# Transposed products with x: both parts of x in one instruction, the halves added by the taker

## The chip, the cores and the metric

The kernel runs as one program on one core of a Trainium2 chip. Its time is the device time of one execution, in microseconds (us). The time before is the median of three runs; the profile comes from one more execution. The engines are PE (TensorE: matrix products), DVE (VectorE), ACT (ScalarE), POOL (GpSimd) and SP (SyncE, which starts transfers).

## The reference

The kernel computes four layers over 256 tokens of width 1024, one batch, all in fp32. The first block has two layers alike, each of a SwiGLU, a mixer and a second SwiGLU, with a layer norm behind each part. The second block has a layer with an S5 mixer and pooling, and one with stick-breaking attention, each followed by a mixture of 16 experts. Cut to what matters here:

```python
def swiglu(x, w_in, w_out):
    h = x @ w_in
    gate, up = h[..., :D_FF], h[..., D_FF:]          # D_FF = 2816
    return (jax.nn.silu(gate) * up) @ w_out

def hybrid_mixer(x, ...):
    h = x @ w_in                                     # dq dk dv sq sk sv
    ...                                              # rope on q and k
    y_diff = diff_attention(dq, dk, dv, ...)         # softmax(..0) - lam * softmax(..1), times v
    y_swa = swa_sink_attention(sq, sk, sv, ...)      # softmax with a sink in a window of 128
    return concatenate([y_diff, y_swa], -1) @ w_out

def first_block(x, ...):
    for l in range(2):
        x = layer_norm(ALPHA * x + 0.5 * swiglu(x, ...), ...)
        x = layer_norm(ALPHA * x + hybrid_mixer(x, ...), ...)
        x = layer_norm(ALPHA * x + 0.5 * swiglu(x, ...), ...)
    return x
```

## The kernel before

**Products in parts.** Each fp32 operand is split into two parts of a shorter type (fp32r), a rounded one (hi) and the rest (lo), and a product a·b is the sum of hi·hi, hi·lo and lo·hi, added up in PSUM. A weight unit is 256 columns of a weight matrix by all 1024 rows: it is loaded by SP into a ring, ACT rounds it (L336) and DVE subtracts to get the rest (L337). The transposed x lies in two tiles, xh and xl (8 x 256 columns each for the eight slices k of 128 rows).

**S and T.** `S` (L386 to L388) computes 128 output columns by 256 tokens, transposed: for each k three matmuls of 256 columns, hi·xh, hi·xl and lo·xh, into one half of a PSUM bank. A unit has two such parts (m = 0, 1), which share one bank. `T` (L399 to L401) multiplies the FFN's inner tile with rows of the second weight: 12 matmuls of 512 columns a round, into four banks of their own (bank_acc). All other products take banks of one pool of four, bank_w, in turn; a bank is reused when its last reader is done.

**FFN.** There are 22 tiles of 128 inner columns. Rounds i = 2 to 20 go the same way in all four FFNs: S for the gate and the up half of tile i, silu on ACT (L574), multiply on DVE (L575), rounding on ACT (L516) and the rest on DVE (L517), and T for tile i-1 on PE. The rows of the second weight are split on ACT and DVE (L373, L378). PE's order is S(i), T(i-1), S(i+1). On DVE the subtractions for unit i+1 (L337) come ahead of the multiply of round i. FFN 4 (the second of layer 2, 860 to 1025 us) carries in its rounds also the preparation of the S5 layer, mostly small operations on DVE and, late, some products on PE. The tail of the FFN handles the last tile token by token (L543, L544, L549).

**Mixer.** Five units go through S (`proj`) and a copy from the bank into a tile qs on ACT (L795, `proj_out`); then rope: one matmul on PE (L803), multiplies on POOL and DVE (L807). Between the projections stand the softmax of the sliding window (scores L829, maximum L842, normalizing L851), the transposes of the probabilities (L817, `at_T`, evacuated on DVE by L114) and their products with v (L860). The order of the calls is written out by hand, and each engine works through its queue in that order.

**Stick-breaking layer.** Eight units go through S (`qk`) and one scaled copy on ACT (L2155).

The S5 layer's tile gyhl and the experts' tile ple lie in the buffers of xl, plain transposed x in that of xh.

Of the kernel before, what the change touches and what calls it, by code (L numbers as in the profile page):

```python
# [8 lines left out]
F32 = mybir.dt.float32  # L9
F32R = mybir.dt.float32r  # L10
BF16 = mybir.dt.bfloat16
I32 = mybir.dt.int32
AF = mybir.ActivationFunctionType
ALU = mybir.AluOpType
# [3 lines left out]
P = 128  # L18
D = 1024
# [63 lines left out]
class K:  # L83
# [117 lines left out]
                between = between()  # L201

    def new_plain_xT(self, xT=None):
        self.xT = xT or self.xp.tile([P, 8, 256], F32, tag="xh", name="xT")

    def new_xT(self):
        self.xh = self.xp.tile([P, 8, 256], F32R, tag="xh", name="xh")
        self.xl = self.xp.tile([P, 8, 256], F32R, tag="xl", name="xl")

    def load_ln(self, g, b):  # L210
        t = self.lp.tile([P, 2, D], F32, tag="lnrow", name="lnrow", bufs=1)
# [166 lines left out]
        (lo_eng or self.nc.vector).tensor_sub(lo, src, f(hi))  # L378
        return hi, lo

    def S(self, out, unit, m):

        hi, lo = unit
        for k in range(8):
            a, b = hi[:, m, k, :], lo[:, m, k, :]
            self.nc.tensor.matmul(out, a, self.xh[:, k, :], start=(k == 0), stop=False)  # L386
            self.nc.tensor.matmul(out, a, self.xl[:, k, :], start=False, stop=False)  # L387
            self.nc.tensor.matmul(out, b, self.xh[:, k, :], start=False, stop=(k == 7))  # L388

    def T(self, acc, st, unit, first, last, tts=(0, 1), hs=(0, 1)):  # L390

# [114 lines left out]
    def ffn(self, row, next_pre, hooks={}):  # L506
        nc = self.nc
        sp = self.sp
        acc = None
        rows = {}  # L510
        queue = []
        new_g = lambda: sp.tile([P, 2, 256], F32R, tag="rt", name="gg", bufs=3)
        new_s = lambda: sp.tile([P, 2, 256], F32, tag="qs", name="sg", bufs=3)

        def split_g(gg, cols, src):
            nc.scalar.copy(gg[:, 0, cols], src)  # L516
            nc.vector.tensor_sub(gg[:, 1, cols], src, f(gg[:, 0, cols]))  # L517

        def down(last=False):
            nonlocal acc  # L520
            i, gg = queue.pop(0)
            if acc is None:
                acc = self.new_acc()
            self.T(acc, (gg[:, 0], gg[:, 1]), rows.pop(i), i == 0, last)
            if i + 2 < NF:
                rows[i + 2] = self.ffn_rows(i + 2)


        u = list(self.pre)
        g2 = [new_g() for _ in range(2)]  # L530
        tok = {}

        def proj(j, tt):
            b = self.bank()[:, :256]
            self.proj_T(b, u[j], tt)
            return b

        def head(j, tt, b=None):
            if b is None:
                b = proj(j, tt)  # L540
            sg = new_s()
            s, g = sg[:, 0, :P], sg[:, 1, :P]
            nc.scalar.activation(s, b[:, 0:P], AF.Silu)  # L543
            nc.vector.tensor_mul(g, s, b[:, P:256])  # L544
            tok[j, tt] = g

        def head_tr(j, tt):
            b = self.bank()[:, :P]
            nc.tensor.transpose(b, tok.pop((j, tt)), self.ident)  # L549
            split_g(g2[j], slice(tt * P, tt * P + P), b)  # L550

        head(0, 0, self.hb[0])
        b01 = proj(0, 1)
        head(1, 0, self.hb[1])
        rows[0] = self.ffn_rows(0)
        head_tr(0, 0)
        head(0, 1, b01)
        head_tr(1, 0)
        nxt = self.ffn_cols(2)
        head(1, 1)  # L560
        rows[1] = self.ffn_rows(1)
        head_tr(0, 1)
        queue += [(0, g2[0]), (1, g2[1])]
        for i in range(2, NF - 1):
            unit = nxt
            nxt = self.ffn_cols(i + 1)
            pg = self.bank()
            for m in range(2):
                self.S(pg[:, m * 256:m * 256 + 256], unit, m)
            if i == 2:  # L570
                head_tr(1, 1)
            sg = new_s()
            s, g = sg[:, 0], sg[:, 1]
            nc.scalar.activation(s, pg[:, 0:256], AF.Silu)  # L574
            nc.vector.tensor_mul(g, s, pg[:, 256:512])  # L575
            gg = new_g()
            split_g(gg, slice(0, 256), g)
            queue.append((i, gg))
            while len(queue) > (2 if i == 2 else 1):
                down()  # L580
            if i in hooks:
                hooks[i]()

        u[0] = nxt
        g2[0] = new_g()
        _, gg = queue.pop()
        before, last = rows.pop(NF - 2), rows.pop(NF - 1)
        units = []

        def part(g, r, tt, h, end):  # L590
            self.T(acc, (g[:, 0], g[:, 1]), r, False, end, (tt,), (h,))

        def over0():
            units.append(self.in_steps(next_pre[0]))
            units[0]("copy", 0.75)
            units[0]("sub", 0.5, nc.gpsimd)

        def over1():
            units[0]("copy")
            units[0]("sub", 1, nc.gpsimd)  # L600
            units[0]("free")
            head(0, 1)
            part(gg, before, 1, 0, False)

        def over2():
            units.append(self.in_steps(next_pre[1]))
            head_tr(0, 1)
            units[1]("copy", 0.25)
            part(gg, before, 1, 1, False)

        def over3():
            units[1]("sub", 0.25, nc.vector)

        def over4():
            part(g2[0], last, 1, 0, True)
            return over4_2

        def over4_2():
            units[1]("copy")
            units[1]("sub", 0.25, nc.gpsimd)  # L620
            part(g2[0], last, 1, 1, True)

        def over5():
            units[1]("sub", 0.25, nc.gpsimd)
            units[1]("sub", 1, nc.vector)
            units[1]("free")

        head(0, 0)
        part(gg, before, 0, 0, False)
        head_tr(0, 0)  # L630
        part(gg, before, 0, 1, False)
        for h in range(2):
            part(g2[0], last, 0, h, True)
        self.layer_norm(acc, True, row() if callable(row) else row, done=self.head,
                        over=(over0, over1, over2, over3, over4, over5))
# [149 lines left out]
        yield u  # L785

    def proj(self, unit):
        b = self.bank()
        for m in range(2):
            self.S(b[:, m * 256:m * 256 + 256], unit, m)  # L790
        return b

    def proj_out(self, b):
        qs = self.sp.tile([P, 2, 256], F32, tag="qs", name="qs", bufs=3)
        self.nc.scalar.copy(qs.rearrange("p m t -> p (m t)"), b)  # L795
        return qs

    def rope(self, qs, dst, cos, sin):
# [561 lines left out]
    def s5_layer(self, wk, sc, projected, row, head, scanned):  # L1360

        nc = self.nc
        V, G = nc.vector, nc.gpsimd
        mm = nc.tensor.matmul
# [7 lines left out]
        S = [sc.tile([P, 2, 4, 65], F32, name=f"S{i}") for i in range(4)]  # L1372
# [173 lines left out]
        vproj(1, 1)  # L1546
        projected()
        scan(3)
        yhl = self.xp.tile([P, 2, 4, 256], F32R, tag="xl", name="gyhl")
        yh, yl = yhl[:, 0], yhl[:, 1]  # L1550
        for g in range(4):
            pooled(g)
        for g in range(4):
# [29 lines left out]
        g = self.rows_units()  # L1583
# [3 lines left out]
        for mp in range(2):  # L1587
            b = self.bank()
            for m in range(2):
                o = b[:, m * 256:m * 256 + 256]  # L1590
                for k in range(4):
# [8 lines left out]
                                   op0=ALU.add, op1=ALU.mult)  # L1600
# [94 lines left out]
    def moe_head(self, l):  # L1695


        nc = self.nc
        mm = nc.tensor.matmul

        class H:
# [15 lines left out]
            def proj(h, tt, halves=(0, 1)):  # L1717

                if tt == 0 and 0 in halves:
                    self.ple = self.xp.tile([P, 2, D], F32, tag="xl", name="ple")  # L1720
                    h.ip, W = self.ring.take()
                    h.pw = W[:, :2 * D].rearrange("p (k c) -> p k c", k=2)
                out = []
                for i in halves:
                    c, op = slice(512 * i, 512 * i + 512), self.bank()
                    out.append((c, op))
                    for k in range(2):
                        mm(op, h.pT[:, k, tt * P:tt * P + P], h.pw[:, k, c], start=(k == 0), stop=(k == 1))
                if tt == 1 and 1 in halves:
                    self.ring.free(h.ip)  # L1730

                def rest():
                    for c, op in out:
                        nc.scalar.activation(self.ple[:, tt, c], op, AF.Copy, scale=0.5)
                return rest
# [388 lines left out]
    def sb_layer(self, wk, sc, projected, row, head, scored):  # L2124

        nc = self.nc
        V, G = nc.vector, nc.gpsimd
        mm = nc.tensor.matmul
        v = sc.tile([P, 2, D], F32, name="sbv")
        yh = wk.tile([P, 8, 256], F32R, name="sbyh")  # L2130
# [17 lines left out]
        vproj(3, 1)  # L2148

        def qk(unit, scale):  # L2150
            b = self.bank()
            for m in range(2):
                self.S(b[:, m * 256:m * 256 + 256], unit, m)
            t = sc.tile([P, 2, 256], F32, tag="qk", name="qk", bufs=6)
            nc.scalar.activation(t.rearrange("p m t -> p (m t)"), b, AF.Copy, scale=scale)  # L2155
            return t

        def scores(q, k, m):
# [322 lines left out]
```

## Time and profile before

| what | us |
|---|---|
| three runs | 1792.59, 1797.18, 1796.63 |
| median | 1796.63 |
| the profiled execution | 1793.23 |
| its span | 1791.5 |
| busy in the span: PE, DVE, ACT, POOL | 1704.7, 929.0, 712.7, 348.2 |
| S: 4512 matmuls of 256 columns | 1270.6 |

The profiled execution is 1.7 us longer than its span, which runs from the first to the last recorded instruction. Busy time is the sum of an engine's records, of which those of PE overlap one another: a matmul's record reaches past the start of the next. So the distance between starts tells how long a stream of matmuls takes, and the mean of a record does not. A share of busy time is a mean over stages of different kinds; the windows and timelines below look at single stages. The mean clock granted to PE in the profiled execution was 0.989 of full speed.

### The profile page before, as it was taken

Reading aid. Unit: us, or ns where it says so; the run is one execution under the profiler, and the core shown is the slowest. Engines: PE = TensorE matmul, PEld = TensorE weight load, DVE = VectorE, ACT = ScalarE, POOL = GpSimd, SP = SyncE. Lnnn points to the kernel's source line nnn. Section 1 sums busy time; section 2 is a strip of 40 time slices with the busy share of each in tenths; the row PEclk is TensorE's granted clock in tenths of the full one; section 3 lists DMA queues with packets and bytes.
Section 4 is the critical chain, followed back from the end, with each engine's and each line's share of the span. In section 5 each row is a group of like instructions: output and inputs, shape, how many; then the busy total and the mean of one; then the engine's idle time right before and its main releaser. Section 6 shows DMA issues by size and latency. Waiting matters only on the chain. (4 is left out here: it accounts for less than half of the span.)

```text
span 1791.5 us, 27789 instructions
## 1 busy us (share of the span) xinstructions
PE 1704.7 (95%) x11407; PEld 1328.9 (74%) x11407; DVE 929.0 (52%) x1523; ACT 712.7 (40%) x1256; POOL 348.2 (19%) x403
## 2 busy tenths in 40 slices
PE   9999998999999999998999988899998999899997
PEld 7999886899989998867999887445453987445443
DVE  5654677655475546677677776432222534422223
ACT  5444456444454444465444435312111465212111
POOL 1000464200020002637061064200000213100001
PEclk9999999999999999999999999999999999999999
DMA  8755442565646555525454556699998737599994
GB/s 286 226 186 195 148 135 87 172 210 167 211 150 209 177 194 165 150 87 153 154 200 152 194 198 257 235 414 414 410 420 322 244 133 289 222 414 414 411 419 184
DMA packets 189483, 421.45 MB, mean 235 GB/s; under 512 B 7264, under 2 KB 142736, under 8 KB 165280
## 3 DMA queue, kind: packets, MB, share of 16 engines
q1 hardware_dynamic: 184848, 405.82, 62.4%
q0 software_dynamic: 3920, 12.95, 2.5%
q8 instruction: 94, 1.54, 0.4%
q10 hardware_dynamic: 576, 0.77, 0.1%
q14 instruction: 45, 0.37, 0.1%
HBM read 418.47 MB, written 1.05 MB: 234 GB/s over the span
## 5 line engine op out<-in xcount | busy, mean ns | idle before, releaser
L386 PE MATMUL bank_w<-xh,unit 128*128 128x256 f32 x1504 | 425.8, 283 | 0.5 <-DVE sg L575 0.5
L388 PE MATMUL bank_w<-xh,unit 128*128 128x256 f32 x1504 | 422.6, 281 | 0.1
L387 PE MATMUL bank_w<-xl,unit 128*128 128x256 f32 x1504 | 422.2, 281 | 0.0
L337 DVE TENSOR_TENSOR unit<-ring,unit 128x1024 fp32r<-128x1024 f32 (+2 forms) x220 | 270.4, 1266 | 51.4 <-ACT unit L336 47.3
L386 PEld LDWEIGHTS bank_w<-xh,unit 128*128 128x128 f32 x1504 | 283.2, 188 | 4.5 <-issue 1.0
L387 PEld LDWEIGHTS bank_w<-xl,unit 128*128 128x128 f32 x1504 | 283.4, 188 | 3.1 <-issue 0.5
L388 PEld LDWEIGHTS bank_w<-xh,unit 128*128 128x128 f32 x1504 | 283.3, 188 | 0.3 <-DVE unit L337 0.3
L336 ACT CAST unit<-ring 128x1024 fp32r<-128x1024 f32 (+2 forms) x297 | 248.5, 891 | 11.1 <-DMA ring<-in_ffn_w_in_dram 10.9
L337 POOL TENSOR_TENSOR unit<-ring,unit 128x512 fp32r<-128x512 f32 (+1 forms) x77 | 113.3, 1488 | 628.9 <-ACT unit L336 628.9
L1902 PE MATMUL bank_w<-ring,xg 128*64 128x512 f32 x1024 | 223.2, 593 | 0.0
L378 DVE TENSOR_TENSOR rl<-ring,rh 128x1024 fp32r<-128x1024 f32 x104 | 129.8, 1249 | 167.3 <-ACT rh L373 167.0
L1902 PEld LDWEIGHTS bank_w<-ring,xg 128*64 128x64 f32 x1024 | 74.2, 137 | 139.8 <-issue 139.0
L373 ACT CAST rh<-ring 128x1024 fp32r<-128x1024 f32 x108 | 113.1, 1049 | 110.2 <-PE bank_acc L401 110.2
L399 PE MATMUL bank_acc<-rh,gg 128*128 128x512 f32 x352 | 139.3, 396 | 0.0
L401 PE MATMUL bank_acc<-rh,gg 128*128 128x512 f32 x352 | 138.5, 394 | 0.0
L400 PE MATMUL bank_acc<-rl,gg 128*128 128x512 f32 x352 | 138.4, 393 | 0.0
L1952 PE MATMUL bank_w<-ring,hT 128*64 128x512 f32 x512 | 113.4, 595 | 2.1 <-issue 2.1
L1916 DVE CAST ohT<-bank_w 128x256 fp32r<-128x256 f32 x16 | 6.8, 425 | 191.9 <-PE bank_w L1912 191.9
L259 POOL TENSOR_SCALAR s_ld<-s_m,s_mu 128x1 f32<-128x1 f32 x20 | 16.6, 832 | 434.0 <-DVE s_mu L250 433.9
L574 ACT ACTIVATE sg<-bank_w 128x256 f32<-128x256 f32 x76 | 29.2, 384 | 172.5 <-PE bank_w L388 172.5
L1952 PEld LDWEIGHTS bank_w<-ring,hT 128*64 128x64 f32 x512 | 38.0, 137 | 68.3 <-issue 66.7
L1960 ACT CAST yhl<-bank_w 128x512 fp32r<-128x512 f32 x32 | 18.7, 586 | 147.3 <-PE bank_w L1952 147.3
(502 smaller groups left out, 2592.2 us busy)
## 6 DMA issues: line engine op xcount, KB each, us to landing
ring<-in_moe_w_dram SPq DMA_DIRECT2D x188, 1024.0 KB, 13.8
ring<-in_ffn_w_in_dram SPq DMA_DIRECT2D x86, 1024.0 KB, 6.6
ring<-in_ffn_w_out_dram SPq DMA_DIRECT2D x44, 1024.0 KB, 5.1
ring<-in_w_in_dram SPq DMA_DIRECT2D x18, 1024.0 KB, 5.8
ring<-in_sb_w_qkv_dram SPq DMA_DIRECT2D x12, 1024.0 KB, 11.3
ring<-in_ple_w_gate_dram SPq DMA_DIRECT2D x8, 1024.0 KB, 18.1
ring<-in_w_out_dram SPq DMA_DIRECT2D x8, 512.0 KB, 6.1
ring<-in_w_out_dram SPq DMA_DIRECT2D x4, 1024.0 KB, 5.2
```

The costliest lines, as they stand in the source:

```text
L336: copy = lambda sel=sel, src=src: self.nc.scalar.copy(sel(hi), src)
L337: sub = lambda eng=eng, sel=sel, src=src: eng.tensor_sub(sel(lo), src, f(sel(hi)))
L373: (copy or self.nc.scalar.copy)(hi, src)
L378: (lo_eng or self.nc.vector).tensor_sub(lo, src, f(hi))
L386: self.nc.tensor.matmul(out, a, self.xh[:, k, :], start=(k == 0), stop=False)
L387: self.nc.tensor.matmul(out, a, self.xl[:, k, :], start=False, stop=False)
L388: self.nc.tensor.matmul(out, b, self.xh[:, k, :], start=False, stop=(k == 7))
L399: mm(acc[tt][h], a, hi[:, cols], start=first, stop=False)
L400: mm(acc[tt][h], a, lo[:, cols], start=False, stop=False)
L401: mm(acc[tt][h], b, hi[:, cols], start=False, stop=last)
L1902: nc.tensor.matmul(b[64 * e:64 * e + 64], xg[:, 4 * kh + k, c0 + 64 * e:c0 + 64 * e + 64], ws[e][0][:, 512 * k:512 * k + 512], start=(kh = ...
L1952: nc.tensor.matmul(yb[h][64 * e:64 * e + 64], hT[:, jj, 64 * e:64 * e + 64], w, start=(jj == 0), stop=(jj == 3))
```

## The change

`S` takes a whole bank per part m. Per k it issues one matmul of 512 columns, hi times both parts of x side by side, and one of 256 columns, lo·xh, added into the bank's first half. The bank then holds two halves, whose sum is the result. Who takes the result adds them: `halves` copies the second half on ACT and adds the first on DVE. FFN: two such pairs per round ahead of silu and multiply, which now read SBUF; mixer: two pairs in place of one copy; stick-breaking: two scaled copies on ACT and two multiply-adds on DVE in place of one scaled copy. The tiles xh and xl become one tile xx, so that one instruction can read both, and the tiles that shared their buffers move into it. 94 units (76 in the FFNs, 10 in the mixers, 8 in the stick-breaking layer) go through S, each with 2 parts of 8 k.

```diff
@@ -201,11 +201,16 @@
                 between = between()
 
     def new_plain_xT(self, xT=None):
-        self.xT = xT or self.xp.tile([P, 8, 256], F32, tag="xh", name="xT")
+        if xT is None:
+
+            t = self.xp.tile([P, 2, 2048], F32, tag="xx", name="xTs")
+            self.sums = t[:, 1].rearrange("p (t c) -> p t c", t=2)
+            xT = t[:, 0].rearrange("p (k t) -> p k t", k=8)
+        self.xT = xT
 
     def new_xT(self):
-        self.xh = self.xp.tile([P, 8, 256], F32R, tag="xh", name="xh")
-        self.xl = self.xp.tile([P, 8, 256], F32R, tag="xl", name="xl")
+        self.xx = self.xp.tile([P, 2, 8, 256], F32R, tag="xx", name="xx")
+        self.xh, self.xl = self.xx[:, 0], self.xx[:, 1]
 
     def load_ln(self, g, b):
         t = self.lp.tile([P, 2, D], F32, tag="lnrow", name="lnrow", bufs=1)
@@ -378,14 +383,21 @@
         (lo_eng or self.nc.vector).tensor_sub(lo, src, f(hi))
         return hi, lo
 
-    def S(self, out, unit, m):
+    def S(self, unit, m):
 
         hi, lo = unit
+        mm = self.nc.tensor.matmul
+        out = self.bank()
         for k in range(8):
-            a, b = hi[:, m, k, :], lo[:, m, k, :]
-            self.nc.tensor.matmul(out, a, self.xh[:, k, :], start=(k == 0), stop=False)
-            self.nc.tensor.matmul(out, a, self.xl[:, k, :], start=False, stop=False)
-            self.nc.tensor.matmul(out, b, self.xh[:, k, :], start=False, stop=(k == 7))
+
+            mm(out, hi[:, m, k, :], self.xx[:, :, k, :], start=(k == 0), stop=False)
+            mm(out[:, :256], lo[:, m, k, :], self.xh[:, k, :], start=False, stop=(k == 7))
+        return out
+
+    def halves(self, dst, b):
+
+        self.nc.scalar.copy(dst, b[:, 256:512])
+        self.nc.vector.tensor_add(dst, dst, b[:, 0:256])
 
     def T(self, acc, st, unit, first, last, tts=(0, 1), hs=(0, 1)):
 
@@ -564,15 +576,15 @@
         for i in range(2, NF - 1):
             unit = nxt
             nxt = self.ffn_cols(i + 1)
-            pg = self.bank()
-            for m in range(2):
-                self.S(pg[:, m * 256:m * 256 + 256], unit, m)
+            pg = [self.S(unit, m) for m in range(2)]
             if i == 2:
                 head_tr(1, 1)
             sg = new_s()
             s, g = sg[:, 0], sg[:, 1]
-            nc.scalar.activation(s, pg[:, 0:256], AF.Silu)
-            nc.vector.tensor_mul(g, s, pg[:, 256:512])
+            for t, b in zip((s, g), pg):
+                self.halves(t, b)
+            nc.scalar.activation(s, s, AF.Silu)
+            nc.vector.tensor_mul(g, s, g)
             gg = new_g()
             split_g(gg, slice(0, 256), g)
             queue.append((i, gg))
@@ -785,14 +797,12 @@
         yield u
 
     def proj(self, unit):
-        b = self.bank()
-        for m in range(2):
-            self.S(b[:, m * 256:m * 256 + 256], unit, m)
-        return b
-
-    def proj_out(self, b):
+        return [self.S(unit, m) for m in range(2)]
+
+    def proj_out(self, bs):
         qs = self.sp.tile([P, 2, 256], F32, tag="qs", name="qs", bufs=3)
-        self.nc.scalar.copy(qs.rearrange("p m t -> p (m t)"), b)
+        for m, b in enumerate(bs):
+            self.halves(qs[:, m], b)
         return qs
 
     def rope(self, qs, dst, cos, sin):
@@ -1546,8 +1556,8 @@
         vproj(1, 1)
         projected()
         scan(3)
-        yhl = self.xp.tile([P, 2, 4, 256], F32R, tag="xl", name="gyhl")
-        yh, yl = yhl[:, 0], yhl[:, 1]
+        yhl = self.xp.tile([P, 2, 2, 4, 256], F32R, tag="xx", name="gyhl")
+        yh, yl = yhl[:, 1, 0], yhl[:, 1, 1]
         for g in range(4):
             pooled(g)
         for g in range(4):
@@ -1717,7 +1727,7 @@
             def proj(h, tt, halves=(0, 1)):
 
                 if tt == 0 and 0 in halves:
-                    self.ple = self.xp.tile([P, 2, D], F32, tag="xl", name="ple")
+                    self.ple = self.sums
                     h.ip, W = self.ring.take()
                     h.pw = W[:, :2 * D].rearrange("p (k c) -> p k c", k=2)
                 out = []
@@ -2148,11 +2158,11 @@
         vproj(3, 1)
 
         def qk(unit, scale):
-            b = self.bank()
-            for m in range(2):
-                self.S(b[:, m * 256:m * 256 + 256], unit, m)
+            bs = self.proj(unit)
             t = sc.tile([P, 2, 256], F32, tag="qk", name="qk", bufs=6)
-            nc.scalar.activation(t.rearrange("p m t -> p (m t)"), b, AF.Copy, scale=scale)
+            for m, b in enumerate(bs):
+                nc.scalar.activation(t[:, m], b[:, 256:512], AF.Copy, scale=scale)
+                V.scalar_tensor_tensor(t[:, m], b[:, 0:256], scale, t[:, m], op0=ALU.mult, op1=ALU.add)
             return t
 
         def scores(q, k, m):
```

DVE in FFN 4, the round at 908 to 913 us; before, from the subtractions of the next weight unit to the first operation of the S5 hook:

```order
L337 TENSOR_TENSOR unit<-ring,unit 128x1024 x2
L575 TENSOR_TENSOR sg<-sg,bank_w 128x256
L517 TENSOR_TENSOR gg<-sg,gg 128x256
L378 TENSOR_TENSOR rl<-ring,rh 128x1024
L1222 TENSOR_TENSOR t_8995<-rql 128x16
L1223 TENSOR_TENSOR t_8996<-rql 128x16
```

and in the changed kernel (its lines are numbered anew: L342 is the subtraction, L400 the add, L587 the multiply):

```order
L342 TENSOR_TENSOR unit<-ring,unit 128x1024 x2
L400 TENSOR_TENSOR sg<-sg,bank_w 128x256 x2
L587 TENSOR_TENSOR sg<-sg 128x256
L529 TENSOR_TENSOR gg<-sg,gg 128x256
L383 TENSOR_TENSOR rl<-ring,rh 128x1024
L1232 TENSOR_TENSOR t_8198<-rql 128x16
L1233 TENSOR_TENSOR t_8199<-rql 128x16
```

Two adds stand between the unit's subtractions and the multiply; the S5 operations behind keep their order.

DVE in the first mixer, from the subtractions of a weight unit to the first score maximum (nsink_: the sinks; pT: the transposed probabilities); before:

```order
L337 TENSOR_TENSOR unit_2510<-ring_2211,unit_2509 128x512 x2
L807 TENSOR_TENSOR rt_2574<-bank_w_2572,sin_683 128x512
L114 COPY pT_2590<-bank_w_2585 128x512
L842 TENSOR_REDUCE s_nm_2602<-bank_acc_2592 128x2
L843 TENSOR_SCALAR s_nm_2602<-s_nm_2602,nsink0_1026 128x2
```

and after:

```order
L342 TENSOR_TENSOR unit_2263<-ring_2000,unit_2262 128x512 x2
L400 TENSOR_TENSOR qs_2308<-qs_2308,bank_w_2274 128x256
L400 TENSOR_TENSOR qs_2308<-qs_2308,bank_w_2291 128x256
L817 TENSOR_TENSOR rt_2315<-bank_w_2313,sin_638 128x512
L114 COPY pT_2331<-bank_w_2326 128x512
L852 TENSOR_REDUCE s_nm_2343<-bank_acc_2333 128x2
L853 TENSOR_SCALAR s_nm_2343<-s_nm_2343,nsink0_937 128x2
```

Two adds have come between the subtractions and the rotary multiply; pT still comes from the second head's transposes, now in bank_w_2326.

PE at the same place of the first mixer, the last products of the projection whose halves lie in bank_w_2274 and bank_w_2291, the rotary product, the transposes of two heads and the scores behind them:

```order
L393 MATMUL bank_w_2291<-xx_1835,unit_2168 128x512
L394 MATMUL bank_w_2291<-xx_1835,unit_2169 128x256
L813 MATMUL bank_w_2313<-qs_2215,consts_76 128x512
L827 MATMUL bank_w_2319<-consts_76,prob_2239 128x128 x4
L827 MATMUL bank_w_2326<-consts_76,prob_2243 128x128 x4
L839 MATMUL bank_acc_2333<-sk_1949,sq_1948 128x256
L839 MATMUL bank_acc_2334<-sk_1949,sq_1948 128x256
```

Before, the same place read:

```order
L387 MATMUL bank_w_2521<-xl_2046,unit_2403 128x256
L388 MATMUL bank_w_2521<-xh_2045,unit_2404 128x256
L803 MATMUL bank_w_2572<-qs_2465,consts_76 128x512
L817 MATMUL bank_w_2578<-consts_76,prob_2486 128x128 x4
L817 MATMUL bank_w_2585<-consts_76,prob_2490 128x128 x4
L829 MATMUL bank_acc_2592<-sk_2160,sq_2159 128x256
L829 MATMUL bank_acc_2593<-sk_2160,sq_2159 128x256
```

The order on PE is the same; the banks differ. Since four banks go in turn, the fourth after bank_w_2274 in the order of use, bank_w_2326, is the same memory.

## Rows read from the trace of the kernel before

**Rows 1.** The page: busy time by engine, and the matmul groups of both widths.

```profile
PE 1704.7 (95%) x11407; PEld 1328.9 (74%) x11407; DVE 929.0 (52%) x1523; ACT 712.7 (40%) x1256; POOL 348.2 (19%) x403
...
L386 PE MATMUL bank_w<-xh,unit 128*128 128x256 f32 x1504 | 425.8, 283 | 0.5 <-DVE sg L575 0.5
...
L399 PE MATMUL bank_acc<-rh,gg 128*128 128x512 f32 x352 | 139.3, 396 | 0.0
```

**Rows 2.** PE timeline, FFN 1: start us, us, engine line op.

```profile
107.41 0.40 PE L399 MATMUL bank_acc<-rh,gg 128*128 128x512 f32 x1
...
110.18 0.28 PE L386 MATMUL bank_w<-xh,unit 128*128 128x256 f32 x1
...
115.86 0.40 PE L399 MATMUL bank_acc<-rh,gg 128*128 128x512 f32 x1
```

**Rows 3.** DVE timeline, the same FFN: idle before in brackets.

```profile
111.50 1.23 DVE L378 TENSOR_TENSOR rl<-ring,rh 128x1024 fp32r<-128x1024 f32 x1 [2.15 <-ACT rh L373]
...
116.47 0.42 DVE L575 TENSOR_TENSOR sg<-sg,bank_w 128x256 f32<-128x256 f32 x1 [1.48 <-ACT sg L574]
117.36 0.42 DVE L517 TENSOR_TENSOR gg<-sg,gg 128x256 fp32r<-128x256 f32 x1 [0.47 <-ACT gg L516]
```

**Rows 4.** ACT groups by form: silu of one half, copy of two.

```profile
L574 ACT ACTIVATE sg<-bank_w 128x256 f32<-128x256 f32 x76 | 29.2, 384 | 172.5 <-PE bank_w L388 172.5
...
L795 ACT COPY qs<-bank_w 128x512 f32<-128x512 f32 x10 | 5.9, 590 | 20.5 <-PE bank_w L388 11.1 <-issue 9.4
```

**Rows 5.** Busy time by engine in one window: us of 165, FFN 4.

```profile
860.00:1025.00 165.00, 163.15 (x1328) 151.67 (x1327) 123.62 (x243) 71.20 (x102) 38.56 (x61) 1.00 0.50 167
```

**Rows 6.** ACT timeline, FFN 4: when the silu could start.

```profile
882.41 0.38 ACT L574 ACTIVATE sg<-bank_w 128x256 f32<-128x256 f32 x1 [2.68 <-PE bank_w L388]
```

**Rows 7.** DVE timeline, FFN 4, first run of S5 work.

```profile
882.52 2.36 DVE L337 TENSOR_TENSOR unit<-ring,unit 128x1024 fp32r<-128x1024 f32 x2
884.79 0.41 DVE L575 TENSOR_TENSOR sg<-sg,bank_w 128x256 f32<-128x256 f32 x1
...
893.76 0.41 DVE L575 TENSOR_TENSOR sg<-sg,bank_w 128x256 f32<-128x256 f32 x1
...
902.95 0.41 DVE L575 TENSOR_TENSOR sg<-sg,bank_w 128x256 f32<-128x256 f32 x1
...
912.45 1.22 DVE L378 TENSOR_TENSOR rl<-ring,rh 128x1024 fp32r<-128x1024 f32 x1 [0.53 <-ACT rh L373]
...
933.50 0.42 DVE L575 TENSOR_TENSOR sg<-sg,bank_w 128x256 f32<-128x256 f32 x1
```

**Rows 8.** DVE timeline, FFN 4, second and third run of S5 work.

```profile
955.31 0.41 DVE L575 TENSOR_TENSOR sg<-sg,bank_w 128x256 f32<-128x256 f32 x1
...
983.58 0.42 DVE L575 TENSOR_TENSOR sg<-sg,bank_w 128x256 f32<-128x256 f32 x1
...
1002.87 0.42 DVE L575 TENSOR_TENSOR sg<-sg,bank_w 128x256 f32<-128x256 f32 x1
...
1024.40 0.28 DVE L544 TENSOR_TENSOR sg<-sg,bank_w 128x128 f32<-128x128 f32 x1
```

**Rows 9.** PE waits: waiting tile and line, releaser, us in total, times, longest.

```profile
PE bank_w L549 <- DVE sg L544: 2.6, 5, 1.3
```

**Rows 10.** PE timeline, first mixer: transposes and the scores behind them.

```profile
246.71 1.04 PE L817 MATMUL bank_w<-consts,prob 128*128 128x128 f32 x8
247.67 0.70 PE L829 MATMUL bank_acc<-sk,sq 64*128 64x256 f32 x4
```

**Rows 11.** DVE timeline, first mixer: unit, transposed tile, score maxima.

```profile
246.22 3.43 DVE L337 TENSOR_TENSOR unit<-ring,unit 128x512 fp32r<-128x512 f32 x2
...
250.17 0.67 DVE L114 COPY pT<-bank_w 128x512 f32<-128x512 f32 x1
250.77 0.68 DVE L842 TENSOR_REDUCE s_nm<-bank_acc 128x2 f32<-128x512 f32 x1
...
260.97 0.68 DVE L842 TENSOR_REDUCE s_nm<-bank_acc 128x2 f32<-128x512 f32 x1
```

## The prediction

> **What bounds the kernel now.** I read the page first: TensorE (PE) is busy for 95% of the span, the vector engine (DVE) for 52% and the scalar engine (ACT) for 40% [rows 1], so at first sight only PE counts. The two groups of matmuls there seem to promise much: 283 ns for one of 256 columns and 396 ns for one of 512, so two of 256 would cost 170 ns more than one of 512. The PE timeline says otherwise, because these records overlap; what counts is the distance from start to start. In FFN 1 twelve 512-column matmuls start between 107.41 and 110.18 us, 230.8 ns apart, and forty-eight of 256 columns between 110.18 and 115.86 us, 118.3 ns apart [rows 2]. Two of 256 take 236.7 ns, hardly more than one of 512. One FFN round, 12 T matmuls and 48 S matmuls, is 2.77 + 5.68 = 8.45 us of PE without a gap.
>
> Next I read DVE's timeline for each stage, since the change gives it work. In a plain FFN round DVE stands still for 2.15, 1.48 and 0.47 us [rows 3]. In FFN 4, which also prepares the S5 layer, it is busy for 123.6 of 165 us [rows 5], and long stretches hold only the two short breaks of about 0.5 us in a round (rows 3 and 7 show one each). In the mixers the row from the weight part to the score maximum is without a break too [rows 11]. There the end is set by DVE's queue and not by the matmuls.
>
> **The change, part by part.**
>
> *PE.* A step over k had 3 x 118.3 = 354.9 ns and gets 230.8 + 118.3 = 349.1 ns, 5.8 ns less. The starts are given to 0.01 us, which with twelve 512-column matmuls leaves about 0.8 ns each; a 512-column product with the two parts of x lying apart is not in the trace. The lower bound is no gain (it costs what two of 256 cost), the upper about 9 ns if 512 columns run at 228. I take 5.8, since the neighbours in the same stretch are the nearest rows. A unit (2 parts x 8 k) gains 0.093 us; 1504 steps gain 8.7 us [rows 1, 2].
>
> A rule speaks for less. The row of 256 columns shows 118.3 ns and that of 512 230.8. The Trainium skill (TensorE: Matmul & The Clock Gate, section "Back-to-back issue gap") gives N/2.4 + 2.5 ns for a matmul by itself, which is 109.2 and 215.8 ns: an estimate by it is 2.6 ns a step and 3.9 us in all. The trace disagrees with both figures, by 9 and 15 ns, and the rows decide.
>
> *The sum of the halves.* A 128x256 vector instruction with a bank as operand lasts 0.42 us [rows 3], so two adds are 0.84 us a unit for DVE. ACT gets two copies of half a bank: not in the trace, bounded by the silu of half a bank (0.384 us) from below and the copy of a whole one (0.590 us) from above [rows 4]; I take 0.38, which is the same form. In an FFN the multiply used to follow at once when DVE was late; now two adds come first, and silu waits for the first of them on the other engine. Silu (0.38 us) runs beside the second add (0.42 us), so a late DVE loses about 0.9 us a round.
>
> *FFN 1 to 3.* A round's DVE has 4 us of breaks [rows 3] for 0.9 us, and T takes the new tile one round later. The cover holds: 3 x 19 x 0.093 = -5.3 us.
>
> *FFN 4.* 15 of its 19 rounds keep their gain on PE: -1.4 us. Against it stand three runs of S5 work. First run: silu starts at 882.41 [rows 6] and would let the multiply start 0.42 us later, but DVE does it at 884.79, 1.96 us late, after the subtractions of the next weight unit (2.36 us for two parts) [rows 7]. PE needs the first part's low half only 2.89 us after S ended; S ends 0.61 us before a punctual multiply [rows 2, 3], and that half is ready 1.18 us before the multiply. So PE notices when the multiply is 2.89 + 1.18 - 0.61 = 3.46 us late, and the margin is 1.5 us. Multiplies follow at 893.76, 902.95 and, four rounds on, 933.50 [rows 7]: rounds of 8.97, 9.19 and 7.64 us. With 0.9 more against PE's new 8.36 the first costs 1.5 (all the margin), the second 1.7, the others 0.2 each: 2.5 us of waiting. The old kernel caught up in those four; the new one can't. Second run: from 955.31 to 983.58 [rows 8] three rounds of 9.42 us. Their 2.7 us (3 x 0.9) are hidden if the slower rounds behind take them up, or wholly on the path: 0 to 2.7, I take the middle, 1.4. Third run: from 1002.87 to 1024.40 [rows 8] DVE is in its queue up to the product that PE waits for at the FFN's end [rows 9]; three sets of adds stand before it: +2.7. In sum -1.4 + 2.5 + 1.4 + 2.7 = +5.2 us.
>
> *The two mixers.* A projection now holds two of the four banks. In the stage at 246 us PE transposes two heads' probabilities from 246.71 and then does scores from 247.67 [rows 10]. In the new order the second head's transposes go into the bank that held a projection's first half; it comes free with an add, which is queued behind the subtractions of a weight unit (246.22 to 249.65) [rows 11]. So they start at 249.65 + 0.42 = 250.1 instead of 247.2; half a set of transposes (0.5) and scores and mask (0.9) end at 251.5, and with what lies between the scores and the maximum today, about 0.8 us, the score maximum comes at 252.3 instead of 250.77: +1.6. A stage later the same path of 2.7 us from subtractions to maximum stands against some 1.5 before (259.51 to 260.97 [rows 11], the subtraction's end being 10 us later as its maximum is): +1.2 and more. I take +3.0 a mixer; the second runs the same order. Bounds: 0 (a break behind takes it up) and +5 (the wait in each of the four stages). Two mixers: +6.0 us. Their own gain on PE is behind these waits and drops out.
>
> *Stick-breaking layer.* Eight units gain 0.7 us on PE; what waits for the scaled sum gets a vector instruction more. Bounds: -0.7 and, with 0.84 us for each of eight units, +6; DVE has little else there, so I take 0.
>
> POOL's and SP's queues keep their order, and no transfer starts otherwise than by a bank or a tile that comes free.
>
> **Sum.** -5.3 + 5.2 + 6.0 + 0 = +5.9 us. The profiled execution took 1793.2 us (a span of 1791.5 and 1.7 around it), so 1799.1 us. It lies 3.4 us below the median of the runs, 1796.6; the mean of the four times is 1794.9, and from that I forecast 1801 us.
>
> **Rivals.**
>
> *Cover.* DVE's lateness in the mixers and in the first two runs of FFN 4 disappears in breaks, and only the third run pays: -8.7 + 2.7 = -6.0, 1789 us. For it: PE is at 95%, and the old kernel stood such lateness nearly without waits. Against it: the rounds above have no breaks left.
>
> *The change does not do what it says.* A 512-column product with two runs of x costs what two products cost: the gains counted on PE (5.3, 1.4 and 0.7) are gone, the waits stay: 5.9 + 7.4 = +13.3, 1808 us. For it: 230.8 against 236.7 is little. Against it: T's products have the same width and type.
>
> *Banks.* Four banks hold two units; where transposes or S5's products go through the same pool, PE waits for adds behind a weight unit's 2.36 us. It decides where the add comes later than PE's next use: 3 rounds in FFN 4 and 4 stages in each mixer, 11 places at 1 us more than above, +17, 1812 us. Against it: in plain rounds the bank is needed again 8 us later.
>
> *Half.* The mixers hide theirs (+6.0 gone), FFN 4 pays: 1795 us.
>
> *Cheap width.* If, in a stream of loads and products, a wide product came no later than a narrow one, each step would lose 118.3 ns: 178 us less, 1617 us. T's 230.8 ns is such a stream and speaks against it [rows 2]. The Trainium skill (same page and section) states 131 ns as the sustained spacing for 512 columns, little more than the narrow product's distance here; the trace disagrees.
>
> **Chances.** Forecast 0.42, cover 0.25, no gain 0.10, banks 0.12, half 0.09, cheap width 0.02. About 0.3%, 5.4 us, can be told from no change. The forecast's own range, 1795 to 1806, straddles that bound: 0.20 within, 0.22 slower. Cover gives 0.22 faster and 0.03 within; half is within, no gain and banks slower: faster 0.24, same 0.32, slower 0.44. The range from cover less 3 us to banks: 1786 to 1812.
>
> **What would show it.** S's starts: 231 and 118 ns apart. A plain FFN round of 8.36 us. New PE waits in FFN 4 near 900 us for the low half of a unit, a longer wait at its end for the product L556, and in each mixer a wait of the transposes L827 for the add L400. If those waits are missing, the forecast fails on the side of cover; if S's pair is not 349 ns, on the first term.

## The result, and the profile after

The changed kernel takes 1807.07 us (median of 4 runs, 1805.72 to 1809.19) against 1795.41 us (4 runs, 1792.59 to 1797.18): a ratio of 1.0068 with a 95% interval of [1.0048, 1.0087], some 12 us more. Executions of one kernel differ by several us, the longer ones at a lower mean granted clock (17 of the kernel before on one chip: from 1790.98 us at 0.991 to 1799.08 us at 0.983), so where the clock is low in a single trace is partly that execution's. The profiled execution has a span of 1804.0 us, 12.5 above [rows 1]'s. Its page, beside [rows 1]:

```profile
PE 1708.5 (95%) x9903; PEld 1261.8 (70%) x9903; DVE 1001.1 (55%) x1711; ACT 759.3 (42%) x1426; POOL 348.4 (19%) x403
...
L393 PE MATMUL bank_w<-xx,unit 128*128 128x512 f32 x1504 | 534.3, 397 | 1.9 <-DVE sg L400 1.8
L394 PE MATMUL bank_w<-xx,unit 128*128 128x256 f32 x1504 | 423.3, 281 | 2.7 <-DVE unit L342 2.5
```

PE's share is the same, and so are the means of its records, 397 and 281 ns. DVE has 72 us more. Where time went is seen by taking one matmul that stands in both traces and subtracting its start before from its start after; between two such points the difference grows by what a stage lost:

| up to | start before, us | after minus before | the stage |
|---|---|---|---|
| FFN 1 | 205.22 | -2.82 | -2.8 |
| mixer 1 | 304.59 | +1.94 | +4.8 |
| layer norm, start of FFN 2 | 332.33 | +2.91 | +1.0 |
| FFN 2 | 512.04 | +0.38 | -2.5 |
| FFN 3 | 703.47 | -2.19 | -2.6 |
| mixer 2 | 831.06 | +1.46 | +3.7 |
| layer norm, start of FFN 4 | 840.87 | +2.33 | +0.9 |
| FFN 4 | 1031.06 | +11.91 | +9.6 |
| S5 layer | 1104.06 | +11.23 | -0.7 |
| experts 1 | 1402.23 | +12.86 | +1.6 |
| stick-breaking | 1498.51 | +12.43 | -0.4 |
| experts 2 | 1765.82 | +12.60 | +0.2 |

The PE timeline in FFN 1, as [rows 2]:

```profile
105.86 0.40 PE L411 MATMUL bank_acc<-rh,gg 128*128 128x512 f32 x1
...
108.61 0.40 PE L393 MATMUL bank_w<-xx,unit 128*128 128x512 f32 x1
108.84 0.28 PE L394 MATMUL bank_w<-xx,unit 128*128 128x256 f32 x1
108.96 0.39 PE L393 MATMUL bank_w<-xx,unit 128*128 128x512 f32 x1
...
114.16 0.40 PE L411 MATMUL bank_acc<-rh,gg 128*128 128x512 f32 x1
```

Sixteen pairs start between 108.61 and 114.16: 346.9 ns a pair instead of 354.9. A round is 8.30 us instead of 8.45. The waits of PE that are new or longer (waiting tile and line, releaser, us in total, times, longest):

```profile
PE bank_w L827 <- DVE qs L400: 6.4, 4, 2.8
...
PE bank_w L1332 <- DVE sg L400: 3.1, 3, 1.5
PE bank_w L561 <- DVE sg L556: 2.8, 5, 1.4
...
PE bank_w L394 <- DVE unit L342: 2.5, 3, 0.9
...
PE bank_w L393 <- DVE sg L400: 1.8, 1, 1.8
```

L827 are the transposes in the mixers, L1332 products of the S5 layer's preparation in FFN 4; both wait for a bank that an add (L400) sets free. L394's waits, at 905, 932 and 1021 us in FFN 4, are S standing for the low part of its unit. L561 is the product of [rows 9], whose waits sum to 0.2 us more. In mixer 1, DVE and then PE, at the place of [rows 10, 11]:

```profile
242.86 3.42 DVE L342 TENSOR_TENSOR unit<-ring,unit 128x512 fp32r<-128x512 f32 x2
246.20 0.74 DVE L400 TENSOR_TENSOR qs<-qs,bank_w 128x256 f32<-128x256 f32 x2
...
250.68 0.69 DVE L852 TENSOR_REDUCE s_nm<-bank_acc 128x2 f32<-128x512 f32 x1 [2.17 <-PE bank_acc L843]
```

```profile
243.28 0.60 PE L827 MATMUL bank_w<-consts,prob 128*128 128x128 f32 x4
246.66 1.11 PE L827 MATMUL bank_w<-consts,prob 128*128 128x128 f32 x4 [2.78 <-DVE qs L400]
247.71 1.23 PE L839 MATMUL bank_acc<-sk,sq 64*128 64x256 f32 x4
```

The second head's transposes stand still for 2.78 us until the first add is done. Then four score products take 1.23 us, 0.70 in [rows 10]. The windows (busy us of PE, PEld, DVE, ACT, POOL, then the granted clock, DMA share, GB/s) tell why, here and at the next FFN's start; first the changed kernel, then the kernel before:

```profile
246.00:252.00 6.00, 5.33 (x21) 3.32 (x22) 3.52 (x8) 0.27 (x1) 1.27 (x1) 0.55 0.51 178
...
324.00:332.00 8.00, 7.04 (x43) 6.28 (x42) 5.76 (x12) 2.80 (x6) 2.27 (x5) 0.79 0.81 264
```

```profile
246.00:252.00 6.00, 6.00 (x46) 4.54 (x45) 5.96 (x8) 1.55 (x4) 4.39 (x4) 1.00 0.20 42
...
324.00:332.00 8.00, 7.25 (x56) 6.61 (x55) 5.37 (x12) 2.80 (x6) 2.63 (x5) 1.00 0.57 202
```

Behind the wait the granted clock, 0.55 over these 6 us, is near the lower of its two levels (1.2 of 2.4 GHz); before, PE was busy all through the same 6 us at 1.00.

### The profile page after: what moved, and what is told of

Its sections match the earlier page's. It is cut to its first block, busy times and chain, and to the rows that moved or that the text cites. A ratio compares the mean times of both kernels' runs of the same rounds, so it can differ in the third digit from the quotient of the medians.

```text
span 1804.0 us, 25330 instructions
## 1 busy us (share of the span) xinstructions
PE 1708.5 (95%) x9903; PEld 1261.8 (70%) x9903; DVE 1001.1 (55%) x1711; ACT 759.3 (42%) x1426; POOL 348.4 (19%) x403
## 3 DMA queue, kind: packets, MB, share of 16 engines
HBM read 418.47 MB, written 1.05 MB: 233 GB/s over the span
## 5 line engine op out<-in xcount | busy, mean ns | idle before, releaser
L393 PE MATMUL bank_w<-xx,unit 128*128 128x512 f32 x1504 | 534.3, 397 | 1.9 <-DVE sg L400 1.8
L394 PE MATMUL bank_w<-xx,unit 128*128 128x256 f32 x1504 | 423.3, 281 | 2.7 <-DVE unit L342 2.5
L393 PEld LDWEIGHTS bank_w<-xx,unit 128*128 128x128 f32 x1504 | 283.7, 189 | 67.6 <-DVE sg L400 2.0
L342 DVE TENSOR_TENSOR unit<-ring,unit 128x1024 fp32r<-128x1024 f32 (+2 forms) x220 | 269.1, 1259 | 44.3 <-ACT unit L341 41.6
L394 PEld LDWEIGHTS bank_w<-xx,unit 128*128 128x128 f32 x1504 | 284.2, 189 | 8.0 <-DVE unit L342 5.1
L342 POOL TENSOR_TENSOR unit<-ring,unit 128x512 fp32r<-128x512 f32 (+1 forms) x77 | 112.2, 1475 | 636.3 <-ACT unit L341 636.3
L399 ACT COPY sg<-bank_w 128x256 f32<-128x256 f32 x152 | 54.5, 368 | 134.0 <-PE bank_w L394 134.0
L455 PE MATMUL bank_w<-unit,xx 128*128 128x256 f32 x800 | 103.9, 282 | 2.1 <-ACT unit L341 1.4
L455 PEld LDWEIGHTS bank_w<-unit,xx 128*128 128x128 f32 x800 | 98.8, 189 | 6.5 <-ACT unit L341 2.8
L400 DVE TENSOR_TENSOR sg<-sg,bank_w 128x256 f32<-128x256 f32 x152 | 61.4, 416 | 52.1 <-ACT sg L399 52.0
```

The source lines that it names most:

```text
L342: sub = lambda eng=eng, sel=sel, src=src: eng.tensor_sub(sel(lo), src, f(sel(hi)))
L393: mm(out, hi[:, m, k, :], self.xx[:, :, k, :], start=(k == 0), stop=False)
L394: mm(out[:, :256], lo[:, m, k, :], self.xh[:, k, :], start=False, stop=(k == 7))
L455: mm(out, x[:, k, sl], hi[:, :, k, :], start=(i == k == 0), stop=False)
```

## Experiments

Each is shown by its edit; ratios are to the kernel before on the same chip. The narrow form is the old S, three matmuls of 256 columns into one bank, with the old takers.

**Wide S in FFN 1 to 3 alone.**

```diff
+            wide = self.nffn in (1, 2, 3)
-            pg = [self.S(unit, m) for m in range(2)]
+            pg = [self.S(unit, m) for m in range(2)] if wide else self.narrow(unit)
```

> The wide S and its adds only in FFN 1 to 3; FFN 4, the mixers and the stick-breaking layer as before. Queue theory (the loss is DVE's queue: the adds stand behind the subtractions of a weight unit, PE waits for them, and behind some of these waits the granted clock falls): the gain is left alone, about 0.14 us a round in 57 rounds, -8 us, 1787 to 1789, and no new stretch at the low clock. Bank rival (the loss is two of four banks per unit): the same here, since plain rounds reuse a bank 8 us later. If the wide matmul itself were what lowers the clock: low-clock stretches behind FFN 1 to 3 and only -5 us or less.

Measured: 1789.69 us against 1793.40, 0.9978 [0.9969, 0.9987]. By its trace it is 7.3 us ahead at the end of FFN 3 (703 us) and 9.0 at 1050 us; 5.3 are left at the end. That is 3.7 us of the 8 expected. The FFNs do nearly what both theories said, and some of the gain is lost far behind, in stages with the same work (below). That no new stretch at the low clock would come did not hold: the trace has some at 320, 518 and 1050 us. By the expectation's own signs the third theory, that the wide matmul lowers the clock, is thus not ruled out by this run. Another trace speaks against it: the kernel before with POOL's table cut (below) has no wide matmul and still shows a granted clock of 0.50 from 1055 to 1068 us, where the kernel before shows 1.00.

**Wide S in the mixers alone, and in FFN 4 alone.** The same switch.

> The wide S and its adds only in the two mixers. Queue theory and bank rival both: the waits of the transposes for the add (6.4 us in 4) come back, and the low clock at the score stage behind them: +4.8 and +3.7 us as between the two traces, with +1 for the low clock at the following layer norm: +7 to +9 us. My estimate before, without the clock, would be +6.

> The wide S and its adds only in FFN 4. Between the two traces FFN 4 lost 9.6 us and the S5 stage gave 1 to 2 back: +7 to +10 us. Sum of this one, the FFN 1 to 3 one and the mixers one should be +11 to +13, what the whole change costs, if the parts don't depend on one another.

Measured: mixers 1804.50 us, 1.0063 [1.0047, 1.0078], with the wait of L827's line 7.6 us in 4; FFN 4 1806.12 us, 1.0068 [1.0053, 1.0084]. Both cost more than expected: 11.1 us for 7 to 9, and 12.7 for 7 to 10. The trace of FFN 4 alone goes from 1.3 us behind to 10.8 in FFN 4, which is 9.5 as between the two traces, and gets 5 more behind it. The three parts sum to 1.0109, not 1.0068: they aren't independent, as a stage behind gives back or loses up to 5 us.

**The order of adds and subtractions in the mixers.** The whole change, with

```diff
-        d3 = self.plain_unit(GV)
-        q4 = self.proj_out(self.proj(d2))
+        late = self.in_steps(lambda: box.append(self.plain_unit(GV)))
+        late("copy")
+        q4 = self.proj_out(self.proj(d2))
+        late("sub")
```

for each of four units.

> The whole change, but in the mixers the subtractions of the next weight unit are put behind the adds in DVE's queue (the roundings on ACT stay ahead). Queue theory: the 2.8 us wait of the transposes for the add goes, the clock stays up there, and the mixers' loss falls from 8.4 us to 0 to 3: 1797 to 1802 in all; a new wait of the next S for the low part of its unit, below 1 us each, may come. Bank rival: as the whole change, 1807, since the banks are the same.

Measured: 1803.69 us, 1.0058 [1.0043, 1.0074]; between what the two theories expected, and not apart from the whole change by time. In the trace the wait is shorter but not gone, since the adds still stand behind the normalizing of the probabilities in DVE's queue and wait for ACT's copies. PE in mixer 1 and in mixer 2:

```profile
246.14 0.66 PE L870 MATMUL bank_w<-consts,prob 128*128 128x128 f32 x4 [1.79 <-DVE qs L428]
246.72 0.70 PE L882 MATMUL bank_acc<-sk,sq 64*128 64x256 f32 x4
```

```profile
752.92 0.71 PE L870 MATMUL bank_w<-consts,prob 128*128 128x128 f32 x4 [2.08 <-DVE qs L428]
753.56 1.23 PE L882 MATMUL bank_acc<-sk,sq 64*128 64x256 f32 x4
```

This pair bears on the price of the clock. The order is the same and the waits 0.3 us apart; behind the first the scores take 0.70 us and the granted clock is 1.00 (246 to 252 us), behind the second 1.23 us and 0.69 (753 to 764 us). By the starts mixer 1 lost 2.0 us at this stage and mixer 2 5.3; of these, 1.2 come back in mixer 2 at the next set of transposes, where PE waited 1.5 us before for the cast of dv and now waits 0.3. At the mixers' ends 2.1 and 4.1 us are lost. So in this order the queue costs some 2 us a mixer, and the clock behind it 3.3 at the stage and some 2 in the end.

In the order of the whole change each mixer loses 5.1 us from this stage to its end. There the clock and the queue can't be priced apart: with POOL's table cut (below) the granted clock in mixer 1 is 0.86 over 246 to 258 us instead of 0.72, but the next wait for an add is 1.35 us instead of 0.30, and the mixer still loses 4.6.

What makes the clock fall isn't the length of the wait alone. In this same kernel it also fell behind a wait of 1.80 us in FFN 4 (granted clock 0.64 from 940 to 944 us), and in the changed kernel it stayed at 1.00 behind one as long at the same product:

```profile
940.09 0.50 PE L395 MATMUL bank_w<-xx,unit 128*128 128x512 f32 x1 [1.80 <-DVE sg L428]
```

```profile
942.99 0.50 PE L393 MATMUL bank_w<-xx,unit 128*128 128x512 f32 x1 [1.80 <-DVE sg L400]
```

**Two banks without adds.** All S narrow, but

```diff
+        for m in range(2):
+            b = self.bank()[:, :256]
+            self.S_narrow(b, unit, m)
```

> The narrow S as before (three matmuls of 256 columns, no adds), but each part m in a bank of its own, so that a unit holds two of the four banks everywhere; the mixers' and the stick-breaking layer's copies become two of half a bank. Bank theory: the transposes in the mixers and S5's products in FFN 4 wait for a bank as in the whole change: +8 to +12 us. Queue theory: a bank comes free with ACT's copy, silu or the multiply, which in the mixers has nothing queued before it, so the mixers lose at most 1 us; in FFN 4 the bank of the second half is still freed by the multiply behind the subtractions, so up to +3 us there: 0 to +4 in all.

Measured: 1793.64 us against 1794.47, 0.9992 [0.9981, 1.0004]. In its list of PE's waits no bank is waited for that an S result holds; the transposes' wait is that of the kernel before (3.6 us, for the cast of dv). That a unit holds two banks costs nothing if they are freed in time, so banks alone don't explain the loss. In the mixers it takes both, as the orders ahead show: the transposes wait because the bank that comes round to them is the one that a late add must free. Whether late adds would cost anything there with a bank to spare was not run.

**DVE's load without banks.** The kernel before, in FFN 4 alone

```diff
+                    for b in pg:
+                        nc.vector.tensor_add(g, s, b)
                 nc.vector.tensor_mul(g, s, pg[1])
```

> The kernel before, with two more adds of 128x256 on DVE ahead of the multiply in every round of FFN 4 (their result is overwritten by the multiply): DVE's load of the change without its banks, copies and wide matmuls. Queue theory: the first and third run of S5 work lose 2.5 and 2.7 us as I worked out, the second some 1.5: +5 to +8 us, most of the 9.6 that FFN 4 lost, with PE waiting for the low part of a unit. Bank theory: the 3.1 and 1.8 us waits for a bank are what counts, and this one loses below 2 us.

Measured: 1810.27 us, 1.0078 [1.0062, 1.0093]: some 14 to 16 us, where 5 to 8 were expected. By the starts FFN 4 lost 10.6 us (from 0.8 to 11.3 behind), beside 9.5 in the FFN 4 part, which has the gain of PE in it; the rest came behind FFN 4, where the granted clock was 0.52 from 1066 to 1080 us. PE's waits in FFN 4:

```profile
PE bank_w L405 <- DVE sg L624: 2.4, 2, 2.2
...
PE bank_w L407 <- DVE unit L344: 2.2, 3, 0.9
```

S waits for a bank with one bank a unit too: what it waits for is a late DVE. So DVE's load, without the second bank, the copies and the wide matmuls, is enough for FFN 4's loss.

**POOL beside DVE.** By the starts FFN 4 lost 1.9 us between 933 and 954 us (before), for which my sum had nothing, and 2.6 from there to 985. (The 4.5 us in the first expectation below don't come out of the two traces.) DVE there, in the changed kernel, and POOL beside it:

```profile
937.39 1.46 DVE L1307 TENSOR_SCALAR cd<-cre,consts 128x256 f32<-128x256 f32 x2
938.77 1.53 DVE L1307 TENSOR_SCALAR cd<-cim,consts 128x256 f32<-128x256 f32 x2
...
947.92 4.06 DVE L342 TENSOR_TENSOR unit<-ring,unit 128x1024 fp32r<-128x1024 f32 x2
```

```profile
946.88 2.03 POOL L1262 TENSOR_TENSOR s5s<-s5c,ws 128x512 f32<-128x512 f32 x1
948.87 2.03 POOL L1263 TENSOR_TENSOR CT<-s5s,wc 128x512 f32<-128x512 f32 x1
```

The same two operations of POOL in the kernel before, and DVE at that time:

```profile
945.25 1.05 POOL L1252 TENSOR_TENSOR s5s<-s5c,ws 128x512 f32<-128x512 f32 x1
946.26 1.05 POOL L1253 TENSOR_TENSOR CT<-s5s,wc 128x512 f32<-128x512 f32 x1
```

```profile
942.83 0.42 DVE L575 TENSOR_TENSOR sg<-sg,bank_w 128x256 f32<-128x256 f32 x1 [1.55 <-ACT sg L574]
...
946.30 2.10 DVE L378 TENSOR_TENSOR rl<-ring,rh 128x1024 fp32r<-128x1024 f32 x1 [2.15 <-ACT rh L373]
948.32 2.30 DVE L1307 COPY BD<-bb 64x256 f32<-64x256 f32 x4
```

The two subtractions take 2.36 us elsewhere [rows 7]. So POOL's table was cut, in the changed kernel and in that before:

```diff
-                n = min(k, 32)
+                n = 1
```

> The whole change, but POOL's table of the S5 layer's decays is computed for one column in each doubling instead of up to 32 (this leaves most of the table out), so POOL's long operations at 926 to 953 us are gone. In the changed kernel DVE's two subtractions at 947.9 last 4.06 us instead of 2.36, two scalings at 937.4 last 2.99 instead of 1.23, and PE lost 4.5 us between 926 and 954, of which my sum had below 1. Theory that DVE, late by the adds, runs into POOL's long operations and both slow down: those durations return to 2.36 and 1.23, the 1.8 us wait at 941 goes, FFN 4 loses some 6 instead of 9.6, and the time is 3 to 4 us below the whole change's 1807. Rival (the adds' own time is all): durations and time as in the whole change.

> The kernel before with the same cut of POOL's table. There DVE is on time from 933 on, with breaks, so both theories expect no change of time within 0.2% (a short operation of DVE more or less); if it came out 3 us faster, the cut itself would be what helps.

Measured: changed kernel with the cut 1801.26 us, 1.0051 [1.0034, 1.0068]; before with the cut 1.0005 [0.9993, 1.0016]. The same DVE operations with the cut:

```profile
937.57 0.61 DVE L1307 TENSOR_SCALAR cd<-cre,consts 128x256 f32<-128x256 f32 x2
938.10 0.65 DVE L1307 TENSOR_SCALAR cd<-cim,consts 128x256 f32<-128x256 f32 x2
...
945.67 2.36 DVE L342 TENSOR_TENSOR unit<-ring,unit 128x1024 fp32r<-128x1024 f32 x2 [0.69 <-ACT unit L341]
```

The durations came back and the 1.8 us wait of S went. FFN 4 lost 5.7 us up to 1026 (from 3.3 to 9.0 behind) instead of 9.9; nothing was lost from 933 to 954, and 0.7 instead of 2.6 from there to 985. The intervals of the whole times overlap, so the mechanism is shown by the durations and the starts, and its worth, some 3 to 4 us, by the traces. The Trainium skill (Perfetto Trace Analysis, section "Optimizing Scalar/DVE Operations") says that GpSimd and DVE share a read port of SBUF; the rows agree in that both last longer where they meet (4.06 for 2.36 us, 2.03 for 1.05). In the kernel before DVE met POOL too (2.10 us for the 1.23 of [rows 3]), but it had breaks of 1.55 and 2.15 us there to take that up.

**A better version.** Wide S in FFN 1 to 3 and the stick-breaking layer.

> The wide S in FFN 1 to 3 and in the stick-breaking layer; the mixers and FFN 4 as before. Between the traces of before and the change the stick-breaking layer gained about 0.4 us. With FFN 1 to 3 alone the measured gain was 3.7 us, of 8.5 that stood in its trace until the S5 layer. Expected: -4 to -5 us. If what ate the gain of FFN 1 to 3 is low-clock stretches that fall elsewhere in each kernel, this one may come out anywhere from -2 to -9 with the same work.

Measured: 1790.52 us against 1794.47, 0.9972 [0.9961, 0.9984]. It beats both kernels; from FFN 1 to 3 alone it can't be told apart.

**Where the rest of the gain of FFN 1 to 3 went.** In its trace the layer norm behind the first experts starts late, for DVE's own sequencer (DVEq):

```profile
1377.98 0.69 DVE L253 SCALAR_TENSOR_TENSOR lnr<-xTs,bank_acc 128x512 f32<-128x512 f32 x1 [3.14 <-DVEq L2101]
```

To shift DVE's code, 74 tiny writes (`nc.vector.memset(self.padt, 0.0)`) went into the rounds' breaks.

> FFN 1 to 3 wide, as in the first experiment, and 74 tiny writes on DVE (128x16, result unused) behind the rest in the rounds of FFN 1 to 3, where DVE has breaks; so DVE's instruction count is 1711 as in the whole change. In the profiles the layer norm behind the first mixture of experts waits 0.5 to 0.7 us for DVE's sequencer in four kernels and 2.8 to 3.3 in five. Theory that the place of DVE's code decides (how many instructions stand ahead of that loop): this wait falls from 3.1 to about 0.7 us, the following layer norm comes 2.4 us earlier and the time is some 2 us below FFN 1 to 3 alone, -5 to -7 us against before. Rival (the wait follows from when the loop starts, or from the state that the wide matmuls leave): still 3 us there and -3.7 us. FFN 1 to 3 keep -8.5 us in both.

Measured: 1790.89 us against 1793.03, 0.9981 [0.9972, 0.9990]: not better. The wait went from the first experts' end and came up at the second's:

```profile
1377.04 0.69 DVE L254 SCALAR_TENSOR_TENSOR lnr<-xTs,bank_acc 128x512 f32<-128x512 f32 x1 [0.72 <-PE bank_acc L2032]
...
1774.91 0.69 DVE L254 SCALAR_TENSOR_TENSOR lnr<-xTs,bank_acc 128x512 f32<-128x512 f32 x1 [2.75 <-DVEq L2109]
```

So the wait moved with instructions hundreds of microseconds ahead; by what rule, these runs don't settle. The number of DVE instructions doesn't decide it, as the changed kernel has 1711 too and waits 0.7 us at the first end and 0.4 at the second.

The rest of the loss, some 1 us each in the S5 layer and at the first experts' start, was not tried. The granted clock was lower at both. In the S5 layer of FFN 1 to 3 alone, and at the same work before:

```profile
1052.00:1056.00 4.00, 4.00 (x65) 3.88 (x61) 0.90 (x2) 0.00 (x0) 0.00 (x0) 0.50 0.04 15
```

```profile
1060.00:1064.00 4.00, 3.69 (x60) 3.62 (x60) 2.44 (x5) 0.00 (x0) 1.07 (x2) 1.00 0.31 121
```

At the experts' start it was 0.63 (1131 to 1145 us) for 0.76 before (1140 to 1154).

## Why the prediction was half right

- *S.* 5.8 ns a step were forecast; the pair measured 8.0 less, and a whole round 0.14 to 0.15 us less, since T's products came a little closer too. FFN 1 to 3: -7.9 instead of -5.3. The 283 ns records would indeed have misled by far. The spacing by the Trainium skill (TensorE: Matmul & The Clock Gate, section "Back-to-back issue gap") would have been 2.6 ns a step, an estimate; the pair's 8.0 ns disagree with it.
- *Cover in FFN 1 to 3*: right; the gain there is whole.
- *FFN 4*, forecast +5.2, measured +9.6. PE gained 0.7 us up to 893. First run, to 933: waits for the unit's low part of 0.76 and 0.83 us, and +2.9 by the starts (forecast 2.5). Third run: +2.9 (forecast +2.7). The step that failed is between: the second run, "0 to 2.7, I take the middle, 1.4", cost 2.6, nearly all of it on the path, and the 20 us ahead of it, for which the sum has nothing, cost 1.9. The first run's lateness was not made up by 933 but carried DVE into POOL's long operations. I took DVE's durations from a schedule in which it met them in its breaks.
- *Mixers*, forecast +6.0, measured +8.4. The place, the releaser and the wait (2.8 us) came as worked out; the wait a stage later, priced at 1.2 and more, was 0.3 and 0.5 us. What I did not price is the clock behind the first wait.
- *Stick-breaking*: -0.4, in the bounds.
- *Not in the sum*: the low clock at two FFN starts, +1.9, and +1.1 net in S5 and the two expert stages.
- *Rivals.* "Banks" (1812 us) is near the time. Its reason, PE waiting for a bank behind late adds, did come about, but not its price: 11.3 us of such waits were in 8 places (L827 6.4 in 4, L1332 3.1 in 3, L393 1.8 in 1) and not 1 us more in 11, two banks alone cost nothing, and in FFN 4 one bank a unit lost as much. "Cover" and "no gain" fall with the waits and the pair's 347 ns.

So the direction and the main mechanism, DVE's queue, stand, and the sum was half: +5.9 for some 12. That the forecast of 1801 us came as near as 6 us to 1807 owes something to luck: FFN 1 to 3 gained 2.6 us more than forecast, which hid a part of what FFN 4, the mixers and the clock cost beyond the sum.

## What to carry to other kernels

Price an instruction added to a queue by what stands behind it in the worst stage, not by the engine's mean load: here 0.84 us a round was free in three FFNs, which gained 7.9 us, and lost 9.6 us in the fourth. Then ask what the lateness runs into: another engine's long operations, and a wait of PE behind which its clock may be low. Apply such a change only where the taker has breaks.

## What the runs showed that I had not expected

- A DVE subtraction pair of 2.36 us lasts 4.06 beside POOL's 512-column operations, and these 2.03 us each instead of 1.05; with POOL's work cut the pair takes 2.36 again.
- The granted clock fell to near its lower level behind PE waits of 2.08 and 1.80 us and not behind one of 1.79 us in the same kernel, with some 2 us between the two outcomes for a mixer. Low stretches also fell at other places from kernel to kernel with the same work there; by what rule, these runs don't settle.
- The wait of DVE for its sequencer at the end of the experts' loop is 0.4 to 0.7 us in some kernels and 2.8 to 3.3 in others, and with 74 unrelated instructions it was at the other loop.
